# Inverting the 64 x 64 blocks of a delta rule: diagonal blocks of 32 by substitution and one correction product, in place of blocks of 16 and three

## The chip, the cores and the metric

The kernel runs on one core of one Trainium2 chip. The metric is the device time of one execution in microseconds, median of three executions: 1300.46 us before the change (1299.64 to 1304.72). The engines are named as the profile names them: PE is the matrix engine (PEld its weight loads), DVE the vector engine, ACT the scalar engine, POOL the general one, SP the one that issues most DMAs. Each engine works through its own queue in order and waits on semaphores for the others.

## The reference

One decoder layer is computed for a prompt of 512 tokens and for 8 samples of 4 tokens, all in float32 with 1024 channels. `P = h @ w_in` feeds three things: a gated causal convolution of width 31, an RWKV-7 mixer with 16 heads of 64 channels, and two merge gates. After the merge come `w_out`, a feed-forward block of 4096 and the norms. The change touches the RWKV-7 recurrence alone:

```
sk = einsum('bhvk,bhk->bhv', s, kk_t)
s  = s * w_t[:, :, None, :] - sk[..., None] * (kk_t * a_t)[:, :, None, :] + v_t[..., None] * k_t[:, :, None, :]
y  = einsum('bhvk,bhk->bhv', s, r_t)
```

Token by token this is serial. Cut into chunks of 64 tokens, each chunk needs the inverse of `I + N`, where N is a strictly triangular 64 x 64 matrix of that chunk and head.

## The kernel before

The work is written in plain order by Python generators, and a list scheduler of the framework then sets the order of the instructions on each engine by its own estimates; `tc.high_priority(offset=-CP)` puts the convolution last wherever something else is ready. Where two instructions touch the same buffer, semaphores keep them in order.

`w_in` is taken in 58 blocks of 128 columns. Each block is loaded (`raw`), split into a high and a low part (`whi` cast on ACT or POOL at L140, `wlo` by subtraction on DVE at L141), and multiplied in 48 matmuls into the PSUM tile `lin` (L152, three a 128-channel step, two halves of the tokens). These blocks are the filler of the first 650 us: PE works on them while a serial part waits.

The mixer goes over eight pairs of heads. For pair p the code runs, in this written order: the chain over chunks of the pair before (`chain`), the blocks K, R and W of pair p with their evacuations on DVE (tiles `k`, `r`, `v`) and their preparation (`rates`, `front`; tiles `sg`, `kk`, `ap`, `ar`, `bon`), then the second half of `front`, and `inverse`. The stages that matter here are these.

- L553: eight matmuls of 256 columns give the products `pb` of keys and decayed keys; ACT copies their diagonal 32 x 32 blocks to `nd` (L558), DVE masks the rest into `NQ` (L560) and `LR` (L564).
- `inverse`: DVE transposes `nd` to `nt`, which lies in `nw` (L588), so that each partition holds one row of a 32 x 32 block for many blocks. Then comes the substitution, a multiplication into `rt` (L597) and a subtraction from `R` (L599) at each step, every one dependent on the one before. Two transposes give the inverse of the diagonal blocks, `td` and `rd` (L602, L604); ACT copies `td` to `DT64` (L609) and POOL copies `rd` to `D64` (L610).
- `product` (L616): eight matmuls, one a chunk, 64 columns each. The first product, of `NQ` and `DT64`, gives `MT`, the part of the matrix that the diagonal inverse leaves over. Three more apply `x = D64 - MT x`; DVE takes the first two out to `xn` (L630, which lies in `nw`) and the last to `NQ` (L633).
- `chain` uses `NQ`: for each of eight chunks L672, L674, ACT, L679, ACT, L683, ACT; a strictly serial run with `lin` matmuls in its gaps.
- `sample` (L696 to L762) handles the 32 sample tokens of the pair; its small steps alternate PE and DVE (`zn`, `uv`).

The PSUM tile of `pb` has one buffer, shared by L553 and the products; `nd`, `nw`, `R` have one buffer each. So the substitution of pair p+1 starts only when that of pair p is over and its products are taken out.

Of the kernel before, what the change touches and what calls it, by code (L numbers as in the profile page):

```python
# [8 lines left out]
F32 = mybir.dt.float32  # L9
# [3 lines left out]
MULT, ADD, SUB = ALU.mult, ALU.add, ALU.subtract  # L13
# [49 lines left out]
def hybrid_step(ctx: ExitStack, tc: tile.TileContext, xT, hist, s0, win, wco, wro, wo, wup, wdn, lora,  # L63
                vecs, convw, cst, yo, convo, shifto, wkvp, wkvs):
    nc = tc.nc
    PSUM = bass.MemoryType.PSUM
    act = nc.scalar.activation
    tt, stt, ts = nc.vector.tensor_tensor, nc.vector.scalar_tensor_tensor, nc.vector.tensor_scalar
# [45 lines left out]
    def con(name):  # L114
        o = COFF[name]
        return cs[:, o:o + dict(CONSTS)[name]]
# [125 lines left out]
    with tc.tile_pool(name="p0", bufs=1) as p0, tc.tile_pool(name="q0", bufs=1, space=PSUM) as q0:  # L242
        start = tables(LNEXP)
        x = p0.tile([128, KT, N1], F32, name="x")
# [7 lines left out]
        rs, rt = (p0.tile([128, N1], F32, name=n) for n in ("rs", "rt"))  # L252
        hfs = [p0.tile([128, N1], F32, name=f"hf{k}") for k in range(KT)]
        with start:
            for s, (o, m) in enumerate(S1):
                q = slice(o, o + m)
                ps = q0.tile([128, 512], F32, name=f"ss{s}")
# [76 lines left out]
    with ExitStack() as c1:  # L334
        P = lambda name, bufs: c1.enter_context(tc.tile_pool(name=name, bufs=bufs))
        p1 = P("p1", 1)
# [8 lines left out]
        D64 = p1.tile([128, NC, 64], F32, name="D64")  # L345
        DT64 = p1.tile([128, NC, 64], F32, name="DT64")
        MT = p1.tile([128, NC, 2, 64], F32, name="MT")
# [4 lines left out]
        maskD = p1.tile([128, 2, 2, 64], F32, name="maskD")  # L352
        nc.gpsimd.memset(maskD, 0.0)
        maskP = p1.tile([128, 2, 64], F32, name="maskP")
        nc.gpsimd.memset(maskP, 0.0)
        first16 = p1.tile([128, 1], F32, name="first16")
        nc.vector.tensor_reduce(out=first16, in_=con("bmask")[:, 0:4], op=ADD, axis=mybir.AxisListType.X)
        for i in range(2):
            q = slice(64 * i, 64 * i + 64)
            nc.scalar.copy(maskD[q, :, i, :], mask[q].rearrange("p (a t) -> p a t", a=2))  # L360
            nc.scalar.copy(maskP[64 * i:64 * i + 32, i, :], maskS[64 * i:64 * i + 32])
            for g in range(2):
                r, o = slice(64 * i + 32 * g, 64 * i + 32 * g + 32), 32 * g
                nc.gpsimd.memset(maskD[r, 0, i, o:o + 16], 0.0)
                nc.scalar.copy(maskD[r, 0, i, o + 16:o + 32], first16[r].to_broadcast([32, 16]))
        zar = p1.tile([128, NB, 16], F32, name="zar")
        nc.gpsimd.memset(zar, 0.0)
        zbk = p1.tile([128, 2, 64], F32, name="zbk")
# [72 lines left out]
        H = (slice(0, 64), slice(64, 128))  # L441
# [62 lines left out]
        def front(p):  # L504
# [44 lines left out]
            for g in range(2):  # L549
# [11 lines left out]
                for i in range(2):  # L561
# [3 lines left out]
                       in1=mask[z].rearrange("p (a t) -> p a t", a=2).unsqueeze(1).to_broadcast([64, 4, 2, 64]))  # L565
                yield DVE if g else PE
            yield from inverse(p, NQ, nd)

        def value(p):
# [11 lines left out]
        def inverse(p, NQ, nd):  # L581


            nw = p1.tile([128, 1024], F32, name="nw")
            nt = nw.rearrange("p (s t) -> p s t", s=32)
            R = p1.tile([128, 8, 32], F32, name="R")
            nc.scalar.copy(R, con("eye").rearrange("p (j t) -> p j t", j=8))
            nc.vector.transpose(nt.rearrange("p s t -> p t s"),  # L588
                                nd.rearrange("p c t -> p t c").unsqueeze(3).to_broadcast([128, 32, NC, 4]))
            yield DVE  # L590
            half = lambda t, d, o, n: bass.AP(tensor=t.tensor, offset=t.offset + o, ap=[t.ap[0], [d, 2], *n])
            for s in range(15):
                nj, n = s // 4 + 1, 15 - s
                tmp = p1.tile([128, 64], F32, name="rt")
                tv = tmp[:, 0:2 * nj * n].rearrange("p (a j t) -> p a j t", a=2, j=nj)
                rv = half(R, 144, s + 1, [[32, nj], [1, n]])
                tt(out=tv, in0=half(R, 144, s, [[32, nj], [0, n]]),  # L597
                   in1=half(nt, 528, 33 * s + 1, [[0, nj], [1, n]]), op=MULT)
                tt(out=rv, in0=rv, in1=tv, op=SUB)  # L599
                yield DVE  # L600
            td = p1.tile([128, NC, 32], F32, name="td", tag="nd")
            nc.vector.transpose(td.rearrange("p c (j g) -> p j c g", g=4), R.rearrange("p j t -> p (j t)"))  # L602
            rd = p1.tile([128, NC, 32], F32, name="rd", tag="R")
            nc.vector.transpose(rd.rearrange("p c t -> p (c t)"), td.rearrange("p c t -> p (c t)"))  # L604
            yield ACT
            xn = nw[:, T:2 * T].rearrange("p (c t) -> p c t", c=NC)
            for w in range(4):
                q, o = slice(32 * w, 32 * w + 32), 32 * (w % 2)
                nc.scalar.copy(DT64[q, :, o:o + 32], td[q])  # L609
                nc.gpsimd.tensor_copy(D64[q, :, o:o + 32], rd[q])  # L610
                yield (ACT,) if w < 3 else PE

            def product(lhsT, rhs, out):
                ps = qb.tile([128, NC, 64], F32, name="pb", tag="pb")
                for c in range(NC):
                    nc.tensor.matmul(ps[:, c, :], lhsT(c), rhs[:, c, :], start=True, stop=True)  # L616
                    if c % 2 and c < NC - 1:
                        yield
                out(ps)
                yield  # L620

            def to_m(ps):
                for i in range(2):
                    nc.scalar.copy(MT[H[i], :, i, :], ps[H[i]])
            yield from product(lambda c: NQ[:, c, 0], DT64, to_m)
            x = D64
            for it in range(3):
                def to_x(ps):
                    if it < 2:
                        tt(out=xn, in0=D64, in1=ps, op=SUB)  # L630
                    else:
                        for i in range(2):
                            tt(out=NQ[H[i], :, 0, i, :], in0=D64[H[i]], in1=ps[H[i]], op=SUB)  # L633
                yield from product(lambda c: MT[:, c], x, to_x)
                x = xn

        def tokens(p):

# [266 lines left out]
    for j in range(KT):  # L905
        o = page("o")
# [235 lines left out]
```

## Time and profile before

| | us |
|---|---|
| median of three executions | 1300.46 |
| the profiled execution | 1299.37 |
| its span on the core | 1297.6 |
| PE busy | 1238.4 (95%) |
| DVE busy | 819.9 (63%) |
| ACT busy | 652.0 (50%) |
| POOL busy | 198.0 (15%) |

Busy time counts overlapping instructions once, and a matmul's end is modelled, so PE can be called busy while it waits a little. In views of one engine over time, a row gives its start, its duration and the idle time ahead of it with what ended that. Engines overlap the tail of one instruction with the head of the next, so the step from start to start is what an instruction takes of the engine's time; it is shorter than the duration.

### The profile page before, as it was taken

What the parts mean: (1) busy time and instruction counts of PE and PEld (TensorE: products, weight loads), DVE (VectorE), ACT (ScalarE), POOL (GpSimd) and SP (SyncE); (2) the same over time, 40 slices, a digit from 0 to 9 for tenths busy, and PEclk for the clock granted to TensorE, in tenths of its full rate; (3) what the DMA queues carried; (4) which work ended last, traced back from release to release, by engine and by line L of the source; (5) the groups of instructions that cost most, each with busy time, mean ns of one, the idle gap of its engine ahead of it and who ended that gap; (6) DMA issues with size and microseconds to landing.
All of it is one profiled execution on the core that took longest, in us unless ns stands there. A gap on an engine that the chain in (4) does not pass through costs nothing. (4 is left out here: it accounts for less than half of the span.)

```text
span 1297.6 us, 23134 instructions
## 1 busy us (share of the span) xinstructions
PE 1238.4 (95%) x9154; PEld 1162.8 (90%) x9154; DVE 819.9 (63%) x1545; ACT 652.0 (50%) x1563; POOL 198.0 (15%) x286
## 2 busy tenths in 40 slices
PE   7989999999999999999999999999999999999995
PEld 6978888887978888787889999999999999999995
DVE  6889889855888898887677465658432122333345
ACT  7453747575563747538244382356554223554231
POOL 2224232221323233132201100000000000000000
PEclk9989999999999999999999999999999999999998
DMA  6313121120202121131115642361122332232332
GB/s 202 104 33 109 33 82 34 49 69 19 84 33 96 34 81 33 33 95 42 67 48 195 220 167 92 110 209 50 34 82 82 98 86 94 82 97 75 90 98 70
DMA packets 45181, 110.60 MB, mean 85 GB/s; under 512 B 7056, under 2 KB 16528, under 8 KB 45072
## 3 DMA queue, kind: packets, MB, share of 16 engines
q1 hardware_dynamic: 41344, 104.33, 25.6%
q10 hardware_dynamic: 3728, 4.79, 1.1%
q8 instruction: 72, 1.18, 0.4%
q14 instruction: 37, 0.30, 0.1%
HBM read 94.79 MB, written 14.32 MB: 84 GB/s over the span
## 5 line engine op out<-in xcount | busy, mean ns | idle before, releaser
L152 PE MATMUL lin<-xh,whi 128*128 128x272 f32 (+1 forms) x2096 | 616.2, 294 | 4.1 <-DVE r L394 2.0
L152 PE MATMUL lin<-xh,wlo 128*128 128x272 f32 (+1 forms) x2096 | 615.6, 294 | 0.6 <-DVE wlo L141 0.6
L152 PE MATMUL lin<-xl,whi 128*128 128x272 f32 (+1 forms) x2096 | 614.2, 293 | 0.4 <-DVE xl L174 0.2
L152 PEld LDWEIGHTS lin<-xh,whi 128*128 128x128 f32 x2096 | 397.0, 190 | 7.2 <-issue 2.9
L152 PEld LDWEIGHTS lin<-xl,whi 128*128 128x128 f32 x2096 | 396.5, 189 | 3.7 <-issue 1.4
L152 PEld LDWEIGHTS lin<-xh,wlo 128*128 128x128 f32 x2096 | 396.6, 189 | 3.1 <-issue 1.4
L141 DVE TENSOR_TENSOR wlo<-raw,whi 128x1024 fp32r<-128x1024 f32 x131 | 160.7, 1227 | 197.8 <-ACT whi L140 175.7
L292 DVE SCALAR_TENSOR_TENSOR c<-u,cw,c 128x512 f32<-128x512 f32 x240 | 188.0, 783 | 5.7 <-DVE c L292 1.2
L140 ACT CAST whi<-raw 128x1024 fp32r<-128x1024 f32 x76 | 79.7, 1049 | 122.7 <-PE lin L152 119.2
L140 POOL CAST whi<-raw 128x1024 fp32r<-128x1024 f32 x55 | 65.4, 1189 | 319.0 <-PE lin L152 182.9
L152 PE MATMUL lin<-xh,wl 128*128 128x272 f32 x240 | 69.4, 289 | 0.0
L152 PE MATMUL lin<-xl,wh 128*128 128x272 f32 x240 | 69.3, 289 | 0.0
L152 PE MATMUL lin<-xh,wh 128*128 128x272 f32 x240 | 69.2, 288 | 0.0
L1001 DVE TENSOR_TENSOR xl<-ff,xh 128x272 fp32r<-128x272 f32 x64 | 28.3, 442 | 55.9 <-ACT ff L1000 55.9
L687 ACT ACTIVATE SV<-ch,pc 64x64 f32<-64x64 f32 x128 | 39.6, 309 | 19.2 <-PE ch L683 17.8
L228 ACT ACT_TABLE_LOAD x37 | 47.5, 1283 | 1.8 <-PEq L1124 1.2
L152 PEld LDWEIGHTS lin<-xh,wl 128*128 128x128 f32 x240 | 45.2, 188 | 0.1
L152 PEld LDWEIGHTS lin<-xh,wh 128*128 128x128 f32 x240 | 45.2, 188 | 0.1
L152 PEld LDWEIGHTS lin<-xl,wh 128*128 128x128 f32 x240 | 45.1, 188 | 0.1
L681 ACT ACTIVATE SV<-ch 64x64 f32<-64x64 f32 x128 | 27.9, 218 | 33.6 <-PE ch L679 31.6
L760 POOL TENSOR_SCALAR st<-st,epS 128x64 f32<-128x64 f32 x64 | 39.9, 673 | 7.9 <-DVE rt L597 7.9
L998 ACT ACTIVATE ff<-lin 128x272 f32<-128x272 f32 x64 | 25.3, 395 | 29.6 <-PE lin L152 29.5
(274 smaller groups left out, 1830.4 us busy)
## 6 DMA issues: line engine op xcount, KB each, us to landing
raw<-win SPq DMA_DIRECT2D x58, 512.0 KB, 3.7
raw<-wup SPq DMA_DIRECT2D x32, 512.0 KB, 3.6
raw<-wdn SPq DMA_DIRECT2D x32, 512.0 KB, 3.6
g_dr<-g ACTq DMA_DIRECT2D x16, 272.0 KB, 2.9
raw<-wro SPq DMA_DIRECT2D x8, 512.0 KB, 3.7
raw<-wco SPq DMA_DIRECT2D x8, 512.0 KB, 3.6
raw<-wo SPq DMA_DIRECT2D x8, 512.0 KB, 3.6
x<-xT SPq DMA_DIRECT2D x8, 276.0 KB, 4.7
```

Source lines behind the costliest of these rows:

```text
L140: upper(hi, r)
L141: tt(out=lo, in0=r, in1=hi.bitcast(F32), op=SUB)
L152: nc.tensor.matmul(ps, a, b[:, o:o + m], start=k == 0 and i == 0, stop=k == n - 1 and i == 2)
L228: lastact[0] = nc.scalar.preload_act_table_set(name)
L292: stt(out=c[:, 0:T], in0=u[:, t:t + T], scalar=w[:, t:t + 1], in1=c[:, 0:T], op0=MULT, op1=ADD)
L681: nc.scalar.mul(SV[H[i], c, i, :], ch[H[i], 2, B[i]], -1.0)
L687: nc.scalar.mul(SV[H[i], c + 1, i, :], ch[H[i], 1, B[i]], pc[H[i], c:c + 1])
L760: nc.gpsimd.tensor_scalar(st[:, b, :], st[:, b, :], f["epS"][:, b:b + 1], None, MULT)
L998: act(t[:, q], ps, AF.Relu)
L1001: tt(out=lo[:, q], in0=t[:, q], in1=hi[:, q].bitcast(F32), op=SUB)
```

## The change

The diagonal blocks that substitution inverts are 32 x 32, not 16 x 16. A 16 x 16 step worked on both halves of a 32 block at once (`half`, a pattern of two strides); the new one takes the whole block, so that there are 31 steps of two instructions, not 15, on up to 76 elements a partition rather than up to 44. With the 64 block cut in two, `MT` squared is zero, so one correction `D64 - MT D64` is exact and goes straight to `NQ`; the two corrections through `xn` are gone. The mask `maskD` is zero on the whole diagonal 32 block, so `first16` goes.

```diff
-        first16 = p1.tile([128, 1], F32, name="first16")
-        nc.vector.tensor_reduce(out=first16, in_=con("bmask")[:, 0:4], op=ADD, axis=mybir.AxisListType.X)
...
-                nc.gpsimd.memset(maskD[r, 0, i, o:o + 16], 0.0)
-                nc.scalar.copy(maskD[r, 0, i, o + 16:o + 32], first16[r].to_broadcast([32, 16]))
+                nc.gpsimd.memset(maskD[r, 0, i, o:o + 32], 0.0)
...
-            half = lambda t, d, o, n: bass.AP(tensor=t.tensor, offset=t.offset + o, ap=[t.ap[0], [d, 2], *n])
-            for s in range(15):
-                nj, n = s // 4 + 1, 15 - s
-                tmp = p1.tile([128, 64], F32, name="rt")
-                tv = tmp[:, 0:2 * nj * n].rearrange("p (a j t) -> p a j t", a=2, j=nj)
-                rv = half(R, 144, s + 1, [[32, nj], [1, n]])
-                tt(out=tv, in0=half(R, 144, s, [[32, nj], [0, n]]),
-                   in1=half(nt, 528, 33 * s + 1, [[0, nj], [1, n]]), op=MULT)
+            for s in range(31):
+                nj, n = s // 4 + 1, 31 - s
+                tv = p1.tile([128, 80], F32, name="rt")[:, 0:nj * n].rearrange("p (j t) -> p j t", j=nj)
+                rv = R[:, 0:nj, s + 1:32]
+                tt(out=tv, in0=R[:, 0:nj, s:s + 1].to_broadcast([128, nj, n]),
+                   in1=nt[:, s:s + 1, s + 1:32].to_broadcast([128, nj, n]), op=MULT)
                 tt(out=rv, in0=rv, in1=tv, op=SUB)
...
-            x = D64
-            for it in range(3):
-                def to_x(ps):
-                    if it < 2:
-                        tt(out=xn, in0=D64, in1=ps, op=SUB)
-                    else:
-                        for i in range(2):
-                            tt(out=NQ[H[i], :, 0, i, :], in0=D64[H[i]], in1=ps[H[i]], op=SUB)
-                yield from product(lambda c: MT[:, c], x, to_x)
-                x = xn
+            def to_x(ps):
+                for i in range(2):
+                    tt(out=NQ[H[i], :, 0, i, :], in0=D64[H[i]], in1=ps[H[i]], op=SUB)
+            yield from product(lambda c: MT[:, c], D64, to_x)
```

The scheduler makes a new order from this. PE's queue has 8107 matmuls and register rows, not 8235; DVE's has 1786 rows, not 1547. Up to the eight `pb` matmuls of the first pair the order of PE is the one before. Three places differ in a way that matters.

DVE, near the end of the substitution of the first pair, before. `R` and `rt` are the substitution, `c` is the convolution, `k` and `sg` are the second pair's:

```order
L599 TENSOR_TENSOR R<-R,rt 128x2x4x2
L394 SCALAR_TENSOR_TENSOR k<-lin,omu,k 128x268
L597 TENSOR_TENSOR rt<-R,nw 128x8
L141 TENSOR_TENSOR wlo<-raw,whi 128x1024
L599 TENSOR_TENSOR R<-R,rt 128x2x4
L473 SCALAR_TENSOR_TENSOR sg<-cs,sg 128x544
L602 STREAM_TRANSPOSE td<-R 128x8x8x4
```

In both kernels one other row stands behind nearly every row of the substitution; the second pair's preparation has only begun when `td` is reached.

DVE, in the changed kernel, inside the substitution of the first pair (L592 and L594 are its two lines; `kk`, `ap` and the tile `k_1631` are the second pair's preparation):

```order
L73 SCALAR_TENSOR_TENSOR k_1631<-k,k_1631 128x544
L592 TENSOR_TENSOR rt<-R,nw 128x65
L292 SCALAR_TENSOR_TENSOR c<-u,cw,c 128x512
L594 TENSOR_TENSOR R<-R,rt 128x5x13
L141 TENSOR_TENSOR wlo<-raw,whi 128x1024
L592 TENSOR_TENSOR rt<-R,nw 128x60
L497 SCALAR_TENSOR_TENSOR kk<-k,vt,rs 128x544
L594 TENSOR_TENSOR R<-R,rt 128x5x12
L73 SCALAR_TENSOR_TENSOR ap<-ap 128x544
L592 TENSOR_TENSOR rt<-R,nw 128x66
L73 SCALAR_TENSOR_TENSOR ap<-kk,ap 128x544
L594 TENSOR_TENSOR R<-R,rt 128x6x11
```

The rows that prepare the next pair, which stood behind the transposes before, now stand between the steps of the substitution.

PE, from the second product of the first pair on, before:

```order
L616 MATMUL pb<-D_291,MT 128x64 x8
L447 MATMUL aux<-k_1598,cs 128x272
L152 MATMUL lin<-xh,wlo 128x276
L152 MATMUL lin<-xh,whi 128x276
L152 MATMUL lin<-xl,whi 128x276
L152 MATMUL lin<-xh,wlo 128x276
L152 MATMUL lin<-xh,whi 128x276
L616 MATMUL pb<-nw,MT 128x64 x8
```

and in the changed kernel, eleven rows behind the second product (L668, L672, L673 are the chain's L679, L683, L684; L661 to L665 its L672 to L676; L550 is L553, of the second pair):

```order
L152 MATMUL lin<-xh,whi 128x276
L152 MATMUL lin<-xl,whi 128x276
L152 MATMUL lin<-xh,wlo 128x276
L668 MATMUL ch<-xs,NQ 128x128
L550 MATMUL pb<-LR,BK 128x256
L672 MATMUL ch<-SV,BKt 128x128
L673 MATMUL yt<-NQ,SV 128x128
L550 MATMUL pb<-LR,BK 128x256
L661 MATMUL ch<-SV,cs 128x128
L663 MATMUL ch<-SV,LR 128x128
L665 MATMUL yt<-LR,SV 128x128
L550 MATMUL pb<-LR,BK 128x256
```

Before, two more products followed and the next pair's `pb` came late in the chain; now the chain follows the second product and the next pair's `pb` stands in its first steps.

## The prediction, made before the changed kernel ran

> **What bounds the kernel now.** I read the page first: busy times and slices.
>
> ```profile
> span 1297.6 us, 23134 instructions
> PE 1238.4 (95%) x9154; PEld 1162.8 (90%) x9154; DVE 819.9 (63%) x1545; ACT 652.0 (50%) x1563; POOL 198.0 (15%) x286
> PE   7989999999999999999999999999999999999995
> DVE  6889889855888898887677465658432122333345
> ```
>
> PE is busy nearly throughout, DVE eight or nine tenths in the first half only, where the mixer is. So PE time removed counts at once, unless DVE, which gets more work, makes PE wait. I therefore cut the mixer, by the timelines, at two events of each pair: the end of its `pb` matmuls and the start of its first product. Between them runs the substitution (stretch S); from the product to the next pair's `pb` end lies the rest (R). Eight S, seven R, the tail behind the last S; first rows and sums:
>
> ```profile
> 93.10:125.30 32.20, 30.19 (x229) 28.48 (x227) 30.99 (x71) 9.09 (x26) 11.77 (x15) 1.00 0.36 109
> sum 227.10, PE 213.03 PEld 196.76 DVE 202.12 ACT 91.28 POOL 77.02; mean PE 26.63 PEld 24.59 DVE 25.27 ACT 11.41 POOL 9.63
> 125.30:162.60 37.30, 36.23 (x250) 30.82 (x250) 32.93 (x54) 27.23 (x76) 10.65 (x14) 1.00 0.10 29
> sum 319.70, PE 307.66 PEld 265.09 DVE 244.82 ACT 224.40 POOL 84.07; mean PE 43.95 PEld 37.87 DVE 34.97 ACT 32.06 POOL 12.01
> 639.90:1297.60 657.70, 637.90 (x4986) 628.80 (x4986) 302.82 (x497) 283.45 (x561) 14.82 (x14) 0.99 0.33 103
> ```
>
> The columns are length, busy PE, PEld, DVE, ACT, POOL. In S, DVE is busy 202 of 227 us and PE 213: they run neck and neck. In R, DVE has 75 us to spare. PE already waits at the end of S:
>
> ```profile
> PE pb L616 <- ACT DT L609: 7.8, 7, 1.7
> 91.83 1.24 PE L553 MATMUL pb<-LR,BK 128*128 128x256 f32 x5
> 96.75 2.05 DVE L588 STREAM_TRANSPOSE nw<-nd 128x1024 f32<-128x1024 f32 x1
> 123.15 0.41 DVE L602 STREAM_TRANSPOSE td<-R 128x256 f32<-128x256 f32 x1
> 125.30 2.00 PE L616 MATMUL pb<-DT,NQ 128*128 128x64 f32 x16 [0.39 <-ACT DT L609]
> ```
>
> In seven pairs the first product waits for `DT64`, which waits for the substitution. An S stretch has a lead-in of 3.7 us (93.1 to 96.75), the substitution, and 2.15 us from `td` to the product: 5.9 us beside the substitution.
>
> **The change part by part.** Products removed:
>
> ```profile
> L616 PE MATMUL pb<-nw,MT 128*128 128x64 f32 x256 | 31.9, 279 | 0.0
> 131.61 0.29 PE L152 MATMUL lin<-xh,whi 128*128 128x276 f32 x1
> 131.73 1.90 PE L616 MATMUL pb<-nw,MT 128*128 128x64 f32 x16
> 133.44 0.37 PE L152 MATMUL lin<-xl,whi 128*128 128x276 f32 x1
> 133.65 0.29 PE L152 MATMUL lin<-xh,wlo 128*128 128x276 f32 x1
> ```
>
> A product takes PE from 131.73 to 133.44, and the `lin` behind it steps 0.21 instead of 0.13: 1.79 us. Two in each of eight pairs: 16 x 1.79 = 28.7 us off PE.
>
> Substitution:
>
> ```profile
> 111.86 0.18 DVE L597 TENSOR_TENSOR rt<-R,nw 128x36 f32<-128x36 f32 x1
> 111.97 0.70 DVE L299 TENSOR_TENSOR cx<-u,cw 128x496 f32<-128x496 f32 x1
> 120.66 0.15 DVE L597 TENSOR_TENSOR rt<-R,nw 128x8 f32<-128x8 f32 x1
> 120.74 1.21 DVE L141 TENSOR_TENSOR wlo<-raw,whi 128x1024 fp32r<-128x1024 f32 x1
> 121.87 0.16 DVE L599 TENSOR_TENSOR R<-R,rt 128x8 f32<-128x8 f32 x1
> L630 DVE TENSOR_TENSOR nw<-D,pb 128x512 f32<-128x512 f32 x16 | 11.0, 688 | 19.2 <-PE pb L616 19.2
> L292 DVE SCALAR_TENSOR_TENSOR c<-u,cw,c 128x512 f32<-128x512 f32 x240 | 188.0, 783 | 5.7 <-DVE c L292 1.2 <-issue 1.0
> ```
>
> A step takes 0.08 us at 8 elements and 0.11 at 36, so about 0.069 + 0.0011 an element. Before: 30 rows, 880 elements, 3.0 us a pair; after: 62 rows, 3120 elements, 7.7 us (the sizes up to 76 are extrapolated). That is +37 us; L630 goes with some -10: DVE gains 27 us. More weighty is that nearly every one of the 62 rows has another row behind it, mostly a convolution step of 0.67, so the substitution takes what all these rows take. Priced row by row with the trace's steps, `nt` to `td` goes in the eight pairs from 24.1, 21.4, 11.9, 21.4, 21.4, 21.1, 19.3, 10.7 (sum 151.3) to 48.8, 47.6, 17.6, 43.7, 47.8, 48.2, 39.5, 31.7 (sum 324.9).
>
> The scheduler answers by putting more PE work into S. PE's rows, priced likewise (a `lin` 0.125 to 0.128, a 64- or 128-column product of the mixer 0.224): S from 207.2 to 365.8, R from 272.1 to 123.6, the tail from 627.8 to 589.0; 28.7 less in all.
>
> Now the waits. S before took 227.1 us: 8 x 5.9 = 47.2, the rows' 151.3, and 28.6 of things the prices don't hold. One of these is this:
>
> ```profile
> L597 DVE TENSOR_TENSOR rt<-R,nw x120: 148/183/1034, 98.8 to 636.4; 128x24 f32<-128x24 f32 x24, 128x30 f32<-128x30 f32 x16, 128x36 f32<-128x36 f32 x16, 128x28 f32<-128x28 f32 x8
> 117.99 1.57 POOL L140 CAST whi<-raw 128x1024 fp32r<-128x1024 f32 x1 [3.17 <-issue]
> 118.56 1.03 DVE L597 TENSOR_TENSOR rt<-R,nw 128x16 f32<-128x16 f32 x1
> L140 POOL CAST whi<-raw x55: 1032/1047/2602, 33.0 to 732.6; 128x1024 fp32r<-128x1024 f32 x55
> ```
>
> The small row at 118.56 lasts until POOL's cast ends (119.56), nearly six times its median. The other part is waits for the sample steps on PE. For the changed kernel the 28.6 has two ends: it stays (waits come once a pair), or it grows with the work, 28.6 x 324.9/151.3 = 61.4. Holds grow, waits mostly don't: 45, the middle. S is then 324.9 + 47.2 + 45 = 417.1, that is 51.3 beyond PE's 365.8, where it was 19.9 before. Of the PE time saved, 31.4 us comes back as waiting for the substitution.
>
> [...]
>
> R before took 319.7, that is 47.6 beyond its priced 272.1: waits of the products for `DT64`, `MT` and `D64`, and of the serial chain. In the changed kernel two of the four products are gone and half the chain lies in the next S. The 47.6 would be 21.6 in proportion to PE's work, or stays whole if the waits are all in the half that remains; I take 28, 4 a pair, near the proportion, since both causes halve: -19.6.
>
> Edits that cost nothing: `first16` and four small ACT copies ahead of the first pair (cover: PE's order up to its `pb` is unchanged, and `lin` runs there; without cover under 2 us), and wider POOL memsets beside them.
>
> Sum: -28.7 + 31.4 - 19.6 = -16.9 us, against the profiled execution's 1299.4 us (span 1297.6), 1.1 below the median. 1282.5, so 1283 us. Ends: the better ends of both unknowns give -28.7 + 15.0 - 26.0 = -39.7, which counts waits as regained that the chain will still have; the worse give -28.7 + 47.8 + 0 = +19.1, 1318.
>
> **The rivals.** Half a per cent, 6.5 us, is about what a measurement of this kernel can tell from no change.
>
> 1. DVE stays hidden: the waits neither grow nor shrink, and PE gets its 28.7 whole, 1271 us. For it: R has 75 us of free DVE, and the order fills S with PE work. Against it: in S, PE already waits.
>
> 2. No change: S grows as forecast, but R keeps all its 47.6, because the chain's serial latency is now faced with `pb` of the next pair and less filler: -28.7 + 31.4 = +2.7, 1302 us. For it: in the order only six or seven `lin` stand in some of the early chain steps, none in others.
>
> 3. Slower: the next pair's preparation now stands between the steps of the substitution, and DVE works in order. Before, its waits cost idle DVE only:
>
> ```profile
> L473 DVE TENSOR_TENSOR_SCAN sg<-cs,sg 128x544 f32<-128x544 f32 x8 | 10.2, 1281 | 4.8 <-ACT sg L235 4.7
> L73 DVE SCALAR_TENSOR_TENSOR k<-k,k 128x544 f32<-128x544 f32 x8 | 6.6, 827 | 5.2 <-ACT k L490 5.2
> L573 DVE TENSOR_TENSOR bon<-aux,v 128x272 f32<-128x272 f32 x16 | 7.0, 436 | 12.0 <-PE aux L447 11.8
> L432 DVE TENSOR_TENSOR u<-lin,gsg 128x272 f32<-128x272 f32 (+1 forms) x16 | 6.7, 419 | 7.7 <-PE lin L152 7.7
> L500 DVE SCALAR_TENSOR_TENSOR kk<-k,vt,rs 128x544 f32<-128x544 f32 x8 | 6.2, 780 | 2.8 <-ACT rs L235 2.8
> ```
>
> The idle column adds to 32.5 us. If all of it delays the substitution, 1283 + 32.5 = 1315. It decides from 23.4 us on (16.9 + 6.5), some 70% of it. Against it: where DVE is the later engine, what it waits for is ready by then. For it: PE and DVE are so close that each may wait for the other in turn.
>
> That the change doesn't shorten PE's work is excluded by the order: 128 matmuls are gone and none is added.
>
> **How the numbers follow.** The forecast, between 1275 and 1293 us, has 0.42; rival 1 has 0.16, rival 2 (1294 to 1307) 0.22, rival 3 0.20. Faster by over 0.5% is the forecast and rival 1: 0.58; within: 0.22; slower: 0.20. The range 1268 to 1314 takes in rival 1 with 3 us for a product's own waits and reaches almost to rival 3's full price; some 0.12 lies above it and 0.05 below. The forecast's own range is 1275 to 1293.
>
> **What would show it.** PE's products 256 records, not 512. The substitution's rows 248 of each kind, DVE busy some 25 to 40 us more. The wait of the first product for `DT64` (now L604) well above 7.8 us: 20 to 35. The last pair's first product starts later than 639.9, near 93.1 + 417 + 152 = 662 us, and the tail behind it is near 619 instead of 657.7. If that product starts at about 650, rival 1 holds; at 680 or later, the second or third, and DVE's idle column ahead of the next pair's rows tells which: under 15 us the second, above 25 the third. I am wrong altogether if small rows above 44 elements take much more than 0.15 us a step, or if the tail doesn't shorten.

## The result, and the profile after

The changed kernel is slower: 1323.17 us, median of four executions (1319.41 to 1325.37), beside 1302.59 for the kernel before. The ratio is 1.0161 with a 95% interval from 1.0135 to 1.0188. The profiled execution took 1325.01 us, its span is 1323.1. The forecast was 1283 us, and the time lies above its range.

These are the lines of the page that answer to those shown of before: busy times, the slices of PE and DVE, and the granted TensorE clock in tenths.

```profile
span 1323.1 us, 22874 instructions
PE 1238.3 (94%) x8898; PEld 1154.2 (87%) x8898; DVE 851.5 (64%) x1784; ACT 652.5 (49%) x1559; POOL 188.0 (14%) x286
PE   7989899999899898999989879999999999999996
DVE  6789889788978989898861755657533212333345
PEclk9989999999889999998989999999999999999998
```

Of before, the clock row was:

```profile
PEclk9989999999999999999999999999999999999998
```

PE has 256 records fewer, and yet it is busy for as long as before, 1238.3 beside 1238.4 us. The third row says why: the granted clock falls in several slices. The mean granted clock of the span was 0.989 before and is 0.971 now.

The next rows are the cut of the mixer at the same two events of each pair: the stretches S of pairs 0, 2 and 3, the sum of the eight S, the sum of the seven R, the tail. The columns are start and end, length, busy PE, PEld, DVE, ACT, POOL, then the granted clock.

```profile
95.50:156.10 60.60, 56.31 (x413) 53.34 (x411) 57.07 (x141) 24.98 (x61) 21.64 (x27) 0.97 0.27 83
259.60:292.10 32.50, 31.42 (x212) 27.11 (x211) 27.22 (x87) 23.91 (x63) 5.19 (x8) 1.00 0.17 49
317.50:377.10 59.60, 53.76 (x357) 48.23 (x356) 50.06 (x138) 34.63 (x89) 18.82 (x27) 0.91 0.18 55
sum 437.00, PE 401.74 PEld 360.53 DVE 389.01 ACT 243.81 POOL 110.11; mean PE 50.22 PEld 45.07 DVE 48.63 ACT 30.48 POOL 13.76
sum 153.40, PE 147.16 PEld 121.86 DVE 124.51 ACT 76.49 POOL 50.82; mean PE 21.02 PEld 17.41 DVE 17.79 ACT 10.93 POOL 7.26
685.90:1323.10 637.20, 607.28 (x4674) 597.72 (x4674) 268.13 (x450) 280.10 (x551) 5.48 (x8) 0.97 0.32 100
```

S has grown from 227 to 437 us, R has shrunk from 320 to 153, and the tail lost 20 us. In S, DVE is busy 389 of 437 us, as full as before (202 of 227), but for twice the time. Pair 2 shows how much of the length the other rows make: its 62 rows of the substitution are the same, but 87 DVE rows stand in its stretch in all instead of about 140, and the stretch lasts 32.5 us instead of 60.

What PE waits for is new. The first two rows are the same sums, ahead of `bon` and of the key norms, in the kernel before (L447) and after (L444); the last column is PE's idle time ahead of them and what ended it. The other rows are the five whose idle time the third rival counted.

```profile
L447 PE MATMUL aux<-k,cs 128*128 128x272 f32 x64 | 21.8, 423 | 0.0
```

```profile
L444 PE MATMUL aux<-k,cs 128*128 128x272 f32 x64 | 25.7, 487 | 12.6 <-DVE rt L592 7.1 <-DVE k L527 4.0 <-DVE bon L570 1.4
L470 DVE TENSOR_TENSOR_SCAN sg<-cs,sg 128x544 f32<-128x544 f32 x8 | 10.2, 1280 | 0.1
L73 DVE SCALAR_TENSOR_TENSOR k<-k,k 128x544 f32<-128x544 f32 x8 | 6.5, 816 | 0.2 <-ACT k L487 0.2
L570 DVE TENSOR_TENSOR bon<-aux,v 128x272 f32<-128x272 f32 x16 | 6.9, 432 | 5.9 <-PE aux L444 5.9
L429 DVE TENSOR_TENSOR u<-lin,gsg 128x272 f32<-128x272 f32 (+1 forms) x16 | 6.7, 418 | 6.3 <-PE lin L152 6.2
L497 DVE SCALAR_TENSOR_TENSOR kk<-k,vt,rs 128x544 f32<-128x544 f32 x8 | 6.2, 773 | 0.0
```

So DVE's own idle time ahead of those rows fell, from 32.5 to 12.5 us. The rows are ready when DVE comes to them; PE is the one that waits for what stands in DVE's queue. The sums make 12.6 us of PE's additional idle time. Behind the mixer come three more waits for DVE rows (`xl`, `g`, `wlo`), of 4.2, 2.4 and 4.7 us, at 760, 772 and 793 us; before had one of them, of 1.0 us for `g`. One wait for a sum, in pair 4: first the timeline of DVE (start, duration, engine and line), then the sums of that window and what PE sat idle for ahead of them (us, times).

```profile
353.46 0.63 DVE L592 TENSOR_TENSOR rt<-R,nw 128x65 f32<-128x65 f32 x1
354.01 0.18 DVE L73 SCALAR_TENSOR_TENSOR ar<-kk,ep 128x32 f32<-128x32 f32 x1
354.11 1.10 DVE L73 SCALAR_TENSOR_TENSOR kk<-kk,ep 128x512 f32<-128x512 f32 x1
355.13 0.23 DVE L594 TENSOR_TENSOR R<-R,rt 128x65 f32<-128x65 f32 x1
355.28 0.77 DVE L527 SCALAR_TENSOR_TENSOR k<-r,vt,k 128x544 f32<-128x544 f32 x1
```

```profile
L444 PE MATMUL aux<-k,cs x2: 661/727/793, 356.2 to 356.8; 128*128 128x272 f32 x2
its engine sat idle before it (us, times) until:
  DVE rt L592: 3.8, 1
```

The sum at 356.2 needs the `k` that L527 writes, and that row ends at 356.05, with the substitution's rows and the preparation in turn ahead of it. PE sat idle 3.8 us. The profile puts the wait down to `rt`, the row that DVE was at next.

Behind such a wait the clock can fall, in the last pair to 0.50. There the first product waits 3.71 us for `DT64`; the timeline of PE shows it. The two rows behind are, in the columns of the stretches above, the 10.2 us ahead of the wait and the 10.2 us that begin 0.6 us after it.

```profile
681.91 0.29 PE L152 MATMUL lin<-xl,whi 128*128 128x272 f32 x1
685.90 2.56 PE L611 MATMUL pb<-DT,NQ 128*128 128x64 f32 x13 [3.71 <-ACT DT L604]
```

```profile
672.00:682.20 10.20, 10.20 (x81) 9.98 (x80) 9.31 (x30) 1.16 (x3) 2.09 (x2) 1.00 0.37 129
686.50:696.70 10.20, 10.20 (x48) 10.20 (x48) 1.37 (x2) 1.55 (x3) 0.79 (x2) 0.50 0.27 80
```

PE is busy all of both stretches, 81 matmuls in the first and 48 in the second, at a clock of 0.50. In the traces of before and after the clock is either 1.0 or 0.5. Half clock comes there in episodes of 3.41, 6.83 or 10.24 us; leaving out one at the very end, there are 5 of them before (20.5 us in all) and 13 after (68.3 us).

With the mean granted clock c, the span can be split in three parts: idle time of PE (span minus busy), the work lost to the clock, (1 - c) x span, and the work at full clock, which is the rest. It takes PE as busy in the episodes, as it is in the one above; the trace shows that this is not so in all of them, and the lines below the table say what it is worth.

| us | span | PE busy | c | work at full clock | lost to the clock | PE idle |
|---|---|---|---|---|---|---|
| before | 1297.6 | 1238.4 | 0.989 | 1224.1 | 14.3 | 59.2 |
| after | 1323.1 | 1238.3 | 0.971 | 1199.9 | 38.4 | 84.8 |
| difference | +25.5 | -0.1 | | -24.2 | +24.1 | +25.6 |

PE is busy 19.0 of the 20.5 us of episodes before and 60.8 of the 68.3 after, and not at all in the half clock at the very end, which the mean clock holds too. If the loss is counted over busy time alone, it is 9.5 us before and 30.4 after, 20.9 more, and the work is 1228.9 and 1207.9, 21.0 less. The split also counts a microsecond at half clock as half of one of work. In both traces a `lin` matmul with another behind it steps 0.126 us at full clock and 0.227 in the episodes, 1.80 times, in the median, and a `pb` product of 64 columns 0.112 and 0.213, 1.90 times; at the first ratio the 20.9 would be 18.6. So a difference in this split is good to some 3 to 5 us.

Most of the removed products' time did go, but PE waits 25.6 us more, and loses 21 to 24 at half clock.

### The profile page after: what moved, and what is told of

Read it like the earlier page. It is cut to its first block, busy times and chain, and to the rows that moved or that the text cites. A ratio compares the mean times of both kernels' runs of the same rounds, so it can differ in the third digit from the quotient of the medians.

```text
span 1323.1 us, 22874 instructions
## 1 busy us (share of the span) xinstructions
PE 1238.3 (94%) x8898; PEld 1154.2 (87%) x8898; DVE 851.5 (64%) x1784; ACT 652.5 (49%) x1559; POOL 188.0 (14%) x286
## 4 chain that ended last, share of the span: by engine, by line
PE 69%; DVE 15%; ACT 8%; issue 3%; DMA 3%; POOL 1%; SPq 0%; DVEq 0%; ACTq 0%; POOLq 0%
PE lin L152 49%; PE pb L611 2%; ACT SV L676 2%; PE ch L672 2%; PE ch L661 2%; DVE c L292 2%; DVE wlo L141 2%; DVE R L594 2%; DVE rt L592 2%; PE ch L668 2%; ACT SV L670 2%; PE yt L444 1%; DMA raw<-wo 1%; PE aux L715 1%; PE ch L663 1%
## 5 line engine op out<-in xcount | busy, mean ns | idle before, releaser
L152 PE MATMUL lin<-xh,whi 128*128 128x272 f32 (+1 forms) x2096 | 621.5, 297 | 12.5 <-DVE r L391 5.2
L152 PE MATMUL lin<-xh,wlo 128*128 128x272 f32 (+1 forms) x2096 | 624.1, 298 | 6.4 <-DVE wlo L141 6.4
L152 PE MATMUL lin<-xl,whi 128*128 128x272 f32 (+1 forms) x2096 | 623.1, 297 | 4.7 <-DVE xl L174 4.2
L152 PEld LDWEIGHTS lin<-xh,whi 128*128 128x128 f32 x2096 | 401.9, 192 | 18.4 <-issue 7.8
L152 PEld LDWEIGHTS lin<-xh,wlo 128*128 128x128 f32 x2096 | 402.6, 192 | 9.9 <-DVE wlo L141 7.4
L152 PEld LDWEIGHTS lin<-xl,whi 128*128 128x128 f32 x2096 | 402.4, 192 | 8.8 <-DVE xl L174 6.0
L292 DVE SCALAR_TENSOR_TENSOR c<-u,cw,c 128x512 f32<-128x512 f32 x240 | 185.1, 772 | 2.9 <-issue 1.1
L592 DVE TENSOR_TENSOR rt<-R,nw 128x60 f32<-128x60 f32 (+24 forms) x248 | 63.6, 256 | 1.9
L594 DVE TENSOR_TENSOR R<-R,rt 128x60 f32<-128x60 f32 (+24 forms) x248 | 63.5, 256 | 2.0
L676 ACT ACTIVATE SV<-ch,pc 64x64 f32<-64x64 f32 x128 | 39.6, 310 | 28.9 <-PE ch L672 27.7
L228 ACT ACT_TABLE_LOAD x37 | 47.5, 1283 | 1.8 <-PEq L1113 1.2
```

What stands on the lines that cost most here:

```text
L152: nc.tensor.matmul(ps, a, b[:, o:o + m], start=k == 0 and i == 0, stop=k == n - 1 and i == 2)
L228: lastact[0] = nc.scalar.preload_act_table_set(name)
L292: stt(out=c[:, 0:T], in0=u[:, t:t + T], scalar=w[:, t:t + 1], in1=c[:, 0:T], op0=MULT, op1=ADD)
L592: tt(out=tv, in0=R[:, 0:nj, s:s + 1].to_broadcast([128, nj, n]), in1=nt[:, s:s + 1, s + 1:32].to_broadcast([128, nj, n]), op=MULT)
L676: nc.scalar.mul(SV[H[i], c + 1, i, :], ch[H[i], 1, B[i]], pc[H[i], c:c + 1])
```

## The experiments

### The two halves of the change, one by one

With 32 blocks and all four products (the other two correct nothing more):

```diff
 # kernel after
-            yield from product(lambda c: MT[:, c], D64, to_x)
+            x = D64
+            for it in range(3):
...
+                yield from product(lambda c: MT[:, c], x, to_x)
+                x = xn
```

> The changed kernel with the three corrections of before put back (the same values, since the two added ones change nothing): the longer substitution alone. Loop theory (the time from one pair's pb to the next, which the rows that DVE works through between nt and td set, is the bound, not PE's sum): the substitution costs more than its own 37 us of DVE, +45 to +75 over before, 1347 to 1377 us, and S stays near 437. Throughput theory (27 to 37 us more of DVE work, no more): +25 to +40, 1327 to 1342.

Measured: 1361.37 us (1360.06 to 1364.17), ratio 1.0464, interval 1.0439 to 1.0489. S sums to 425.7 us, R to 200.6, the tail is 639.2. The +61 lies in the range of the loop theory.

With 16 blocks and one correction in place of three (for 16 blocks that leaves out part of the inverse):

```diff
 # kernel before
-            for it in range(3):
...
+            yield from product(lambda c: MT[:, c], D64, to_x)
```

> Before with one correction in place of three (two corrections of the blocks of 16 are left out): the removed products alone. If PE's sum is the bound in this half, -28.7, about 1272 us; the loop theory allows a little more, -28 to -38, since two waits of the serial part of each pair go as well; if the products were hidden, no change.

Measured: 1288.59 us (1286.42 to 1291.02), ratio 0.9896, interval 0.9871 to 0.9922. S 229.4, R 304.6, tail 662.0. The gain is 12 us, neither the 28.7 and more of the first two expectations nor nothing.

Beside 1300.45 for before, measured along with them, the longer substitution alone costs 61 us and the removed products alone bring 12. Together they make +21 by the first comparison, not +49: with the long substitution in place the products bring 38, since R is shorter by 47 us (200.6 to 153.5). By the split of the span, the substitution costs the same waits in both kernels that have it, 38 us lost to the clock in each, 90 and 85 us idle. And the products take 30 and 32 us off PE's work, but in the second kernel here the clock fell from 0.989 to 0.975, and 18 us of the 32 went that way (the table below).

### DVE rows that nobody needs

```diff
 # kernel before; called once a pair at the convolution's low priority
+        def extra():
+            eye = con("eye").rearrange("p (j t) -> p j t", j=8)
+            for s in range(16):
+                n = 17 + s % 2
+                rv = nvt[:, 60:60 + 4 * n].rearrange("p (j t) -> p j t", j=4)
+                for op in (MULT, SUB):
+                    tt(out=rv, in0=rv, in1=eye[:, 0:1, 1:1 + n].to_broadcast([128, 4, n]), op=op)
```

> Before with 32 further dependent DVE rows of 68 to 72 elements a pair, of low priority and used by nothing (256 rows, about 37 us of DVE, as many as the longer substitution adds). Throughput theory: +20 to +35 us. Loop theory: the rows go into DVE's idle time outside the substitution, 0 to +8.

Measured: 1320.94 us (1312.13 to 1322.35), ratio 1.0136, interval 1.0098 to 1.0175; S 219.9, R 334.2, tail 660.5. 256 short rows of DVE, on which nothing waits, in the kernel with the short substitution, cost about what the whole change costs, though here R grew and not S; the loop theory's 0 to +8 is out. It fits a cost of DVE's load (40 us more busy) in itself, for which no dependent chain of 62 rows is needed. But the order of all engines is new here too. Two kernels below are 12 and 24 us slower than their partners with fewer rows, or with as many in a new order, so the +20 is not shown to be the load's. The four executions differ by their clock: 0.981 in the one of 1312, 0.973 to 0.977 in the others.

### Convolution rows taken away

The two kernels leave out 29 of the 30 multiply-add rows of each prompt convolution block, 232 of 240 DVE rows. One lasts 0.75 us in the median, in before and in after, not the 0.5 of the expectation below; 59 of the 240 begin in S in before and 141 in after. The convolution's output is another, all else is kept.

```diff
 # in before, and in after
-        for t in range(1, CW):
+        for t in range(1, 2):
```

> The kernel before, leaving out 29 of the 30 multiply-add rows of each prompt convolution block (line L292), 232 DVE rows of about 0.5 us, all in the first 690 us. It is the partner of the next kernel. Theory one (DVE's load sets the stretches of after, PE those of before): a little faster than before, since DVE is off the bound there: 1285 to 1300 us, and the stretch from pb to the first product 205 to 225 us in sum (227). Rival (the substitution's own dependent steps set the stretch): the stretch hardly moves, 220 to 230 us, 1295 to 1302 us.

> The kernel after with the same 232 convolution rows left out. Theory one (after lost because the rows of DVE in the substitution's stretch add up to more than PE's work there): with a quarter of them gone the stretch falls from 437 to 330-370 us, the half-clock time falls under 45 us, and the removed products show: 12 to 28 us faster than the partner, some 1265 to 1280 us. Rival (62 dependent steps at the latency of one each set the stretch, whatever else DVE does): the stretch stays at 415 to 440 us, and the kernel is still 10 to 25 us slower than its partner, 1300 to 1315 us.

Measured: before without them 1312.57 us (1305.06 to 1323.76), ratio to before 1.0079, interval 1.0045 to 1.0113; after without them 1282.34 (1278.68 to 1283.88), ratio 0.9850, interval 0.9819 to 0.9882. With DVE relieved, the change brings 30 us where it cost 21. The sums of S, first of before and then of after without these rows:

```profile
sum 198.90, PE 180.12 PEld 167.07 DVE 165.55 ACT 69.38 POOL 65.90; mean PE 22.51 PEld 20.88 DVE 20.69 ACT 8.67 POOL 8.24
```

```profile
sum 301.60, PE 281.07 PEld 256.32 DVE 259.44 ACT 137.16 POOL 89.11; mean PE 35.13 PEld 32.04 DVE 32.43 ACT 17.14 POOL 11.14
```

S of the changed kernel falls from 437 to 302 us, below the 330 to 370 expected, and the half-clock time from 68.3 to 30.7 us, counted as there; the time lies 2 us above the 1265 to 1280. The 62 dependent steps, which are all there, therefore don't set S, and the rival that they do is out. PE's idle time ahead of the sums goes too, from 12.6 us to 0.2:

```profile
L444 PE MATMUL aux<-k,cs 128*128 128x272 f32 x64 | 21.8, 423 | 0.2 <-DVE ep L476 0.2
```

What was not expected is that before without the rows is slower than before, outside both ranges, though its S fell below the 205 expected. PE's wait for `DT64` grew from 7.8 to 13.8 us, and episodes of 17.1 us (from 650.7) and 10.2 us (from 729.2) stand in its tail. The second goes with this wait; the mean of these `lin` matmuls in that window is 431 ns, beside 296 over the whole of this kernel:

```profile
L152 PE MATMUL lin<-xh,whi 128*128 128x272 f32 x9 | 3.9, 431 | 6.0 <-POOL whi L140 6.0
```

Its executions go from 1305 us at a clock of 0.989 to 1324 at 0.978; against the fastest of them the change would bring 23 us. So part of the 30 is a worse partner and not a better after; after itself gained 41 us by losing the rows.

### The bonus sum fed from another tile

The sums behind `bon` take `v` in place of r*k, so that they don't need L527; the bonus term is thus another.

```diff
 # kernel after
-            f, v, rk = fs[p], pgs["v", p], pgs["k", p]
+            f, v = fs[p], pgs["v", p]
+            rk = v[:, 64:64 + N2]
```

> The kernel after, with one thing changed: the sums at L444 that make `bon` (line L570) take `v` in place of the product r*k (tile `k`, written on DVE at L527 in the midst of the substitution). The output for the bonus term is thus another; the number and size of the instructions stay, but the sum no longer needs the DVE row that stands among the substitution rows. In after PE sat idle 12.5 us ahead of these sums in 7 places, and 17 us at half clock followed three of them (355, 444, 604 us). Theory one (PE starves because the rows it needs stand in the full DVE queue, and the clock falls to half behind each wait): the idle goes, and with it some 8 us of lost half-clock work: 1300 to 1312 us, half-clock time 68 -> about 50 us. Rival (the wait only moves to the next consumer of that DVE queue): 1317 to 1327 us, half-clock time within 10 us of 68.

Measured: 1347.32 us (1345.56 to 1354.03), ratio 1.0355, interval 1.0317 to 1.0393, clock 0.959: slower by 24 us than after, outside both expectations. In some pairs the scheduler put the sums earlier; in pair 4 they stand where they stood, and wait for `v`, which comes off the same DVE queue behind the row of L527. Rows of DVE in pair 4, then what PE sat idle for at these sums (us, times), then the same at the sample's products:

```profile
361.69 0.23 DVE L595 TENSOR_TENSOR R<-R,rt 128x70 f32<-128x70 f32 x1
361.85 0.49 DVE L384 SCALAR_TENSOR_TENSOR v<-lin,omu,v 128x276 f32<-128x276 f32 x1
```

```profile
  DVE v L384: 9.3, 2
```

```profile
  POOL zbk L517: 13.2, 4
```

One of the waits for `v` is 7.07 us long. `zbk` is copied on POOL from `ap`, which DVE writes between two substitution rows, so the second wait comes from the same queue at one remove. The rival, that the wait moves to the next consumer, is right in kind, but it had no price for the new order. Number and size of the instructions are those of after, so the 24 us are the price of a new order and of one moved dependence. That a cause is named does not mean that taking it away is worth its idle time.

### Weight casts on ACT

The interleaved `whi` casts go from POOL to ACT, first in after, then in before.

```diff
 # in after, and in before
-                    ready.append(wsplit(raws[n + 1], upper=nc.gpsimd.tensor_copy))
+                    ready.append(wsplit(raws[n + 1], upper=nc.scalar.copy))
```

> The changed kernel with the upper part of the weight splits on ACT instead of POOL, so that no cast of POOL can hold a row of the substitution. If the holds are the cause: -17 us or more against the changed kernel, under 1306. Loop theory: the holds are one part of S; -5 to -15 if ACT carries the casts at no cost, nothing if ACT's rows then come late.

> The kernel before with the high parts of w_in (`whi`) cast on ACT in place of POOL in the interleaved blocks, the edit that took 13.6 us off after. It is a candidate to beat both. If POOL's casts hold small DVE rows as such: 16 of 240 substitution rows were held by 10.9 us in all, against 26.9 us in after, so a gain in that proportion, 3 to 6 us: 1294 to 1298 us. If the gain in after was of the full DVE queue alone: no change, 1299 to 1303 us. If ACT, 50% busy, becomes the one that PE waits for: slower, 1304 to 1312 us.

Measured: after with it 1309.54 us (1307.41 to 1314.84), ratio 1.0070, interval 1.0044 to 1.0096. Before with it 1286.51 (1282.06 to 1293.40), ratio 0.9883, interval 0.9834 to 0.9932. This is the version that beats both kernels. The edit brings 14 us in each; the 13.6 of after lie in the 5 to 15 of the loop theory. The change costs 23 us in the kernel with casts on ACT, beside 21 in the one without, so the casts are no part of what it costs.

A small substitution row was held in after until a cast of POOL had ended:

```profile
661.53 1.57 POOL L140 CAST whi<-raw 128x1024 fp32r<-128x1024 f32 x1 [6.16 <-issue]
...
662.11 1.07 DVE L592 TENSOR_TENSOR rt<-R,nw 128x69 f32<-128x69 f32 x1
```

39 of the 496 rows of after took over 0.4 us, together 26.9 us beyond 0.185 each; 27 of these ended with a cast and 12 with a copy of POOL (L515). With the casts on ACT 14 did, 6.0 us beyond, all beside those copies. In before it was 16 of 240 and 10.9 us, and none with the casts on ACT. So the holds give 21 and 11 us of DVE time back, and the gain of 14 in before was more than the 3 to 6 expected. Why is not shown: the order is new here as well, and taking convolution rows off DVE did not make this kernel faster. The best kernel's page:

```profile
span 1280.3 us, 23085 instructions
PE 1231.4 (96%) x9154; PEld 1158.5 (90%) x9154; DVE 797.3 (62%) x1545; ACT 702.1 (55%) x1618; POOL 134.7 (11%) x231
PEclk9989999999999999999999999999999999999998
```

### All profiled executions, split in three

| us | span | PE busy | c | work at full clock | lost to the clock | PE idle |
|---|---|---|---|---|---|---|
| 32 blocks, four products | 1358.3 | 1267.9 | 0.972 | 1229.9 | 38.0 | 90.4 |
| before + unused DVE rows | 1310.3 | 1244.3 | 0.981 | 1219.4 | 24.9 | 66.0 |
| before - convolution rows | 1318.8 | 1254.7 | 0.976 | 1223.0 | 31.7 | 64.1 |
| before, casts on ACT | 1280.3 | 1231.4 | 0.993 | 1222.4 | 9.0 | 48.9 |
| 16 blocks, two products | 1289.3 | 1224.0 | 0.975 | 1191.8 | 32.2 | 65.3 |
| after, `bon` from `v` | 1352.2 | 1250.5 | 0.959 | 1195.1 | 55.4 | 101.7 |
| after - convolution rows | 1276.9 | 1214.5 | 0.984 | 1194.1 | 20.4 | 62.4 |
| after, casts on ACT | 1305.6 | 1224.5 | 0.978 | 1195.8 | 28.7 | 81.1 |

The work at full clock is 1219 to 1230 us in the five kernels with four products a chunk (before among them), and 1192 to 1200 in the five with two: 28.4 us apart in the mean, beside the forecast's 28.7. Counted over busy time alone, as above, the groups are 1225 to 1237 and 1199 to 1208, 26.0 apart. What sets one kernel apart from another within a group is in the main idle time and clock.

That the clock costs time, and isn't just a mark of waiting, has a second witness. Executions of one kernel have the same instruction order and differ in clock. Over 64 executions of the ten kernels, each taken against the mean of its own kernel, the time rises by 11.9 us for each 0.01 of clock; 0.01 of a span of 1300 us is 13. It isn't proof, since longer waits would also lower the clock.

## Why the prediction was wrong

**Right.** Products: 256 records, and 26 to 28 us of PE's work by the table above. The prices of the substitution's rows: a row of 76 elements steps 0.148 us (0.153 by the formula), and DVE is busy 31.6 us more, inside the 25 to 40 given. The stretches R: 153.5 us measured, 152 forecast, so that -19.6 stands.

**The extra of S was taken too small.** The step was "Holds grow, waits mostly don't: 45, the middle". From `nt` to `td` the eight substitutions took 386.1 us against 324.9 priced: 61.2, where the proportional end was 61.4. Some 25 us are rows of the substitution held by POOL, 11 before. 36 us are waits of DVE, 14 before, the largest 11 for the sample's sums on PE. So the waits, which were to stay, grew as much in proportion as the holds. More of the sample's and the next pair's rows stand in the stretch; that this is why the waits grew is argued, not shown. The lead-in was 4.2 instead of 3.7 us in seven pairs. S came to 436.9, 20 us above the forecast.

**The tail was taken from PE's order alone.** It was to shorten to 619 us, and is 637.1. The order has less filler there: 95 `lin` matmuls stand among the chain of the last pair instead of 112, and that chain ends at 722 us instead of 678. The three waits at 760 to 793 us come behind it. PE idle in the tail is 29.9 us (637.2 less 607.3) instead of 19.8, and the half-clock time in it, with that at the end, is 32 us instead of 13, up to 10 us more lost. The tail is so 18 us longer than forecast. With 20 from S, 1.5 from R and 2.4 from the start of the first pair, the miss is 42, against 42.5 between the sum's -16.9 and the +25.6 of the profiled execution.

**The step behind both stands in the first paragraph and in the sum:** that PE time removed counts at once unless DVE makes PE wait, and that a wait costs what it lasts. The forecast had 11.8 us of additional waiting (31.4 - 19.6). It was 25.6, and 21 to 24 more were lost to the clock, for which the sum had no term. The clock row of the page before shows the price only as two eights, in the third slice and the last, and the 20.5 us of episodes in its trace were not counted. At the forecast's own waiting, a loss in the same ratio would have been some 10 us, as an estimate from these numbers, and the sum -7.

**The rivals.** The change ended on the third rival's side, at 8 us above its price, but not by its mechanism: DVE's idle column is 12.5 us, below the 15 that was to speak for the second rival. R did shorten, so the second is out as well. The waits are PE's, for rows in DVE's queue, and the place of the wait was wrong too. In S, PE's idle time grew from 14.1 to 35.3 us. But the wait that I named as the sign, that of the first product for `DT64`, fell from 7.8 to 4.1 us instead of rising to 20 to 35. First before, then after, with the weight loads' own wait:

```profile
  PEld pb L616: 9.3, 7
  PE pb L616: 7.8, 7
```

```profile
  PEld pb L611: 6.5, 6
  PE pb L611: 4.1, 2
```

The last pair's first product at 685.9 us told rightly that the second or third rival's side held.

The held rows were borne out: 39 rows of the substitution that took over 0.4 us ended with a cast or copy of POOL in after, 16 with a cast in before, and moving the casts took 14 us off each kernel. Counting half-clock time as half of the work puts the two groups of the table 26 to 28 us apart, beside the forecast's 28.7.

Open: which edit of the order would have kept PE fed in the changed kernel, and how much of the 21 us is the chance of one order. Each edit here moved the scheduler's whole order, so single waits could not be removed one at a time. That DVE's rows set the length of S is shown by the kernels without convolution rows; that the longer S costs time through idle time and half clock is read from the traces.

## What to carry to other kernels

Here PE was 95% busy and DVE nearly as full in the stage that was changed (202 of 227 us), and PE work given up was gained only where DVE had room for what it took on: the change cost 21 us, and brought 30 with 232 DVE rows gone. So with another engine that full, read its busy share in that stage, not over the span. Price a wait of PE at its length and, from 1.5 us on, the half-clock episode that may follow (here behind 25 of the 43 gaps of 1.5 to 2 us): span = work at full clock + lost to the clock + idle is split from three numbers of a profile, and shows to a few us which part an edit moved. And before rows are moved off PE on to DVE, look for small DVE rows held by POOL: here 39 of 496 were, by 26.9 us in all, and a one-word edit brought 14 us, where the change cost 21.

## What the hardware showed that was not expected

Half-clock episodes follow waits of PE that are much shorter than the episodes. In the ten traces, between 30 and 1270 us, these are the idle gaps of PE and PEld together by length, and how many have an episode that begins within the gap or up to 5 us behind it:

| gap, us | 0.1 to 0.5 | 0.5 to 1 | 1 to 1.5 | 1.5 to 2 | 2 to 3 | 3 and more |
|---|---|---|---|---|---|---|
| gaps | 650 | 65 | 37 | 43 | 31 | 33 |
| followed | 9 | 9 | 11 | 25 | 24 | 33 |

All gaps of 3 us and more were followed, over half of those of 1.5 to 2 us, and the episodes last 3.4 to 17.1 us. A gap of 1.18 us in the kernel with 16 blocks and two products has one of 10.2 us behind it. In the traces of before and after the episodes of that time begin and end on one grid of 3.413 us (in after at 686.46 and 696.70 us, 758.14 and 764.97, and so on). With the ten traces cut into windows at that grid, the idle time of PE within one window tells more than the length of a gap. Of the windows at full clock, all 44 with 2 us of idle time or more were followed by one at half clock, 38 of 90 with 1 to 2 us, and 6 of 3352 with less. So the seven gaps of 2 to 3 us that nothing followed each lie across the border of two windows. Taking DVE rows away from before, which made DVE less busy by 170 us, made the kernel slower: where PE waits, and how long at a time, counted there for more than how much another engine has to do.
